# A second store buffer for the attended products of a scan, and their tiles beside its first six blocks

## The chip, the cores and the metric

The kernel runs on one core of a Trainium2 chip. A core has five engines that each work through a queue of their own in order: PE (matrix products), DVE (elementwise work), ACT (activations and copies), POOL (elementwise work and DMA issues) and SP (DMA issues). ACT, POOL and SP each issue DMAs, which run on 16 shared DMA engines. The metric is the device time of one execution in microseconds; the median of three runs stands for a kernel.

## The reference

One layer of a bidirectional encoder on 1024 tokens of width 1024, all in float32. It is two half-step FFNs around a mixer; the mixer projects the input once, gives one part of the columns to dilated window attention (8 heads of 64) and the other to a recurrent group (RWKV-7, 8 heads of 64, forward and backward), and projects both back with one matrix `w_out`:

```python
f = _swiglu(_rmsnorm(h, ffn1_pre_g), ffn1_w_gate, ffn1_w_up, ffn1_w_down)
h = h + 0.5 * _rmsnorm(f, ffn1_post_g)
z = _rmsnorm(h, mix_pre_g) @ w_in
y_att = _attention_group(z[..., :ATT_IN], cos, sin, attn_out_g)
y_rwkv = _rwkv7_group(z[..., ATT_IN:], ...)
mix = jnp.concatenate([y_att, y_rwkv], axis=-1) @ w_out
h = h + _rmsnorm(mix, mix_post_g)
f = _swiglu(_rmsnorm(h, ffn2_pre_g), ffn2_w_gate, ffn2_w_up, ffn2_w_down)
h = h + 0.5 * _rmsnorm(f, ffn2_post_g)
```

The recurrence per head, over time in both directions:

```python
sa = jnp.einsum('dbhvk,dbhk->dbhv', state, kk)
state = state * w[..., None, :] - sa[..., :, None] * kka[..., None, :] + v[..., :, None] * k[..., None, :]
y = jnp.einsum('dbhvk,dbhk->dbhv', state, r)
```

## The kernel before

The kernel runs through the first FFN, the input projection, attention, the recurrent scan, the output projection and the second FFN, in that order, with some work of one stage laid beside another. Products of float32 data are made of three matmuls of a high and a low part (`woh`, `wol` of the weights; `yah`, `yal` of the data), so one product of a 128-row tile with half the output columns takes 4 x 3 = 12 matmuls (`out_products`, L1064).

The scan takes the 1024 steps in 8 blocks, each of which holds two chunks of 64 steps for both directions. For block n there are four pieces of work:

- `prep` (L805 to L846) makes the operands of a block from loads (`th_w`, `th_a`, `in`), with products `lp` and `bp` on PE; it does not depend on the running state.
- `solve` (L854 to L873) inverts a small triangular matrix per head on DVE in 31 pairs of steps (L866, L868); its results `Ti` and `X` go to DRAM from POOL's queue.
- `merge` (L882 to L902) loads those inverses back on POOL's queue and joins them: `pa` on PE, its copies `d` on ACT, `pb` on PE, and the copy `tt` on ACT.
- `chain` (L928 to L972) carries the state through the block: copies `lm` on ACT (L928), then for each chunk `xu` (L941, L952), `xs` (L944), `uv` (L954), `st` and `y` on PE (L937), the new state `sv` on DVE (L968) and the output copy `yb` on ACT (L970). At the end ACT issues the two stores of `yb` to `d_y` (L972).

`run` issues merge(n), chain(n), and then prep and solve of a block three ahead (`upto(n + 3)`). Beside this, `project_attended` multiplies one tile of 128 attended rows with the attended half of `w_out`: load `yat`, scale it on DVE (L1072), transpose it on PE (`yq`, L1075), split it (L1077 on ACT, L1078 on DVE), and for each half of the output columns 12 matmuls `po`, a copy `yao` on ACT (L1083) and a store to the DRAM buffer `d_hp` on ACT's queue (L1084). `yq` and `po` share one bank of PSUM. The weights for it (`WA`) are read and split by `out_weights` in eight pieces of 128 x 512: a load `wor`, a scaled high part `woh` on ACT (L1054) and a low part `wol` on DVE (L1055). `wor` and `yao` are buffers of one tag, "wor", in one pool.

After the last chain, eight `finish_unit` calls (L991 to L1028) load the scan's results (`f_y`, `f_k`, `f_r`, `f_v`, `f_sg`), normalise them (`yc`, `var`, `rstd`, `bonus`, `gate` on PE) and split them. `out_weights` is called a second time for the other half of `w_out`, in another pool, and `out_project` adds the products `pw` (L1064) to the attended part, which it loads from `d_hp`. The second FFN follows.

The order of each engine's queue is set by a scheduler when the kernel is built: it takes the instructions as the program gives them and places them by priority and by the buffers that are free. So the place of a call in `run` and the number of buffers move instructions well beyond the lines themselves.

Of the kernel before, what the change touches and what calls it, by code (L numbers as in the profile page):

```python
# [10 lines left out]
F32 = mybir.dt.float32  # L11
# [8 lines left out]
NK, NT, NJ = D // 128, S // 128, DFF // 128  # L20
# [143 lines left out]
class _Kernel:  # L164
# [876 lines left out]
    def out_weights(self, p, k0, gain=None):  # L1041

        nc, W = self.nc, []
        for k in range(4):
            hl = []
            for dh in range(2):
                raw = p.tile([128, 512], F32, name="wor", tag="wor", bufs=1)
                self.load(raw, self.io["w_out"][0][(k0 + k) * 128:(k0 + k + 1) * 128, dh * 512:(dh + 1) * 512])
                h = p.tile([128, 512], F32R, name="woh", tag="woh", bufs=8)
                l = p.tile([128, 512], F32R, name="wol", tag="wol", bufs=8)  # L1050
                if gain is None:
                    self.split(h, l, raw)
                else:
                    nc.scalar.activation(h, raw, AF.Copy, scale=gain[:, k:k + 1])  # L1054
                    nc.vector.scalar_tensor_tensor(l, raw, gain[:, k:k + 1], h, op0=OP.mult, op1=OP.subtract)  # L1055
                hl.append((h, l))
            W.append(hl)
        return W
# [7 lines left out]
    def project_attended(self, p, c, psum, t, W, rs_a):  # L1066

        nc, V, A, T = self.nc, self.nc.vector, self.nc.scalar, self.nc.tensor
        rows = slice(t * 128, (t + 1) * 128)
        y = p.tile([128, H, 64], F32, name="yat", tag="yat")  # L1070
        self.load(y.rearrange("p a b -> p (a b)"), self.ya_d[rows, :])
        V.tensor_tensor(y, y, rs_a[:, t * H:(t + 1) * H][:, :, None].to_broadcast([128, H, 64]), op=OP.mult)  # L1072
        q = psum.tile([128, 4, 128], F32, name="yq", tag="eo")
        for k in range(4):
            T.transpose(q[:, k, :], y.rearrange("p a b -> p (a b)")[:, k * 128:(k + 1) * 128], self.ident)  # L1075
        h, l = (p.tile([128, 4, 128], F32R, name="ya" + c, tag="ya" + c) for c in "hl")
        A.activation(h, q, AF.Copy)  # L1077
        V.tensor_tensor(l, q, h, op=OP.subtract)  # L1078
        for dh in range(2):
            ps = psum.tile([128, 512], F32, name="po", tag="eo")  # L1080
            self.out_products(ps, W, dh, h, l, slice(0, 128))
            o = p.tile([128, 512], F32, name="yao", tag="wor", bufs=1)
            A.copy(o, ps)  # L1083
            self.nc.scalar.dma_start(self.hp_d[rows, dh * 512:(dh + 1) * 512], o)  # L1084

# [77 lines left out]
    def run(self):  # L1163
# [5 lines left out]
        with self.top as top:  # L1169
# [8 lines left out]
            with ExitStack() as st:  # L1178
# [39 lines left out]
                p = self.pool(st, "ffn1")  # L1218
# [66 lines left out]
            def upto(m):  # L1285
                while nxt[0] <= min(m, NB - 1):
                    n = nxt[0]
                    blk[n] = self.prep(n, sp, pp, (R0, R1, B0)[n % 3])
                    self.solve(n, sp)
                    nxt[0] += 1  # L1290
# [5 lines left out]
            for n in range(NB):  # L1296
                if n:
                    self.merge(n, blk[n], sc, pm)
                self.chain(n, blk.pop(n), sc, pc)
                upto(n + 3)  # L1300
                for t in ([0, 1] if n == 0 else [n + 1] if n + 1 < NT else []):
                    self.project_attended(eo, sc, pe, t, WA, rs_a)
            s_sr.close()
            s_pr.close()
# [27 lines left out]
            for j in range(2):  # L1332
                for n in (1, 2):
                    gate_up.ready[n, j] = self.halves(wf, self.slab(wf, gate_up.source(j, 0, n - 1), bufs=2, queue=nc.gpsimd),
                                                      bufs=4)
# [37 lines left out]
            with ExitStack() as st:  # L1373
# [12 lines left out]
                p, hand = self.pool(st, "ffn2"), self.pool(st, "hand3")  # L1386
# [49 lines left out]
```

## Time and profile before

| what | value |
|---|---|
| runs | 2370.75, 2369.18, 2369.29 us, median 2369.29 |
| span of the profiled execution | 2367.7 us |
| PE busy in it | 2212.2 us (93%) |
| DVE busy | 1782.8 us (75%) |
| ACT busy | 1034.4 us (44%) |
| the eight cycles of the scan, 1280 to 1594 us | 44.7, 53.5, 37.3, 44.3, 38.8, 33.1, 27.2, 35.1 us |
| first tail stretch, 1594 to 1650 us | 56.0 us |

The profile gives no time of the profiled execution apart from its span; the median of the runs is 1.6 us above it. A cycle is counted from the end of the last output copy (`yb`) of one chain to that of the next; cycle 0 begins at 1280 us. In the timelines a row reads: start in us, duration, engine and line, operation, output and input, and in brackets how long the engine had been idle and what released it. PE rows are pipelined, so the busy time of single matmuls can add up to more than the stretch that they take.

### The profile page before, as it was taken

The numbers are of one execution on the slowest core, as the hardware profiler recorded it, in microseconds if no ns is written. First come the engines' busy times: TensorE is split into PE (matmuls) and PEld (weight loads), VectorE is DVE, ScalarE is ACT, GpSimd is POOL, SyncE is SP. The second block draws the span as 40 slices with busy tenths as digits, with TensorE's granted clock in tenths as the row PEclk, the third lists the DMA queues.
The fourth block names the chain that finished last, engine by engine and source line by source line (L and its number), as shares of the span: only waits on it lengthen the run. The fifth ranks groups of instructions, "written<-read, shape, count | busy, mean of one in ns | idle before, by whom it ended". The sixth has DMA issues, their size and how long they took to land. (4 is left out here: it accounts for less than half of the span.)

```text
span 2367.7 us, 39507 instructions
## 1 busy us (share of the span) xinstructions
PE 2212.2 (93%) x14532; PEld 1784.9 (75%) x14532; DVE 1782.8 (75%) x2957; ACT 1034.4 (44%) x1958; POOL 608.7 (26%) x732
## 2 busy tenths in 40 slices
PE   6999999999999998999995889988799999999997
PEld 4788888878877676788774767765678888887886
DVE  8899999865676344667568767837889999987565
ACT  4322333354676413666545545445442333235453
POOL 6244443400000010111102242432334344441000
PEclk8999999999999998999996798989989999999999
DMA  5354445486652514322369676577534544447655
GB/s 156 107 174 151 170 146 170 167 266 193 220 185 98 193 42 134 91 81 71 94 161 223 165 183 176 151 208 256 178 95 168 174 167 154 169 153 265 195 188 181
DMA packets 359381, 386.04 MB, mean 163 GB/s; under 512 B 74258, under 2 KB 265618, under 8 KB 359188
## 3 DMA queue, kind: packets, MB, share of 16 engines
q1 hardware_dynamic: 308512, 276.43, 38.8%
q0 software_dynamic: 30320, 94.44, 11.3%
q10 hardware_dynamic: 20356, 12.66, 1.9%
q8 instruction: 114, 1.87, 0.3%
q14 instruction: 79, 0.65, 0.1%
HBM read 257.53 MB, written 125.89 MB: 162 GB/s over the span
## 5 line engine op out<-in xcount | busy, mean ns | idle before, releaser
L186 ACT ACTIVATE wh<-raw 128x512 fp32r<-128x512 f32 (+1 forms) x273 | 167.8, 626 | 264.1 <-DVE raw L62 95.0
L187 DVE TENSOR_TENSOR wl<-raw,wh 128x512 fp32r<-128x512 f32 (+1 forms) x273 | 277.6, 1020 | 3.1 <-ACT wh L186 2.0
L81 PE MATMUL gu<-xh,wh 128*128 128x512 f32 x704 | 277.9, 395 | 0.9 <-ACT xh L186 0.8
L81 PE MATMUL gu<-xl,wh 128*128 128x512 f32 x704 | 276.3, 393 | 0.0
L81 PE MATMUL gu<-xh,wl 128*128 128x512 f32 x704 | 276.2, 392 | 0.0
L415 PE MATMUL pd<-gl,gwh 128*128 128x512 f32 x616 | 240.4, 390 | 3.1 <-DVE gl L187 3.1
L415 PE MATMUL pd<-gh,gwh 128*128 128x512 f32 x616 | 239.6, 390 | 0.5 <-DVE row L86 0.5
L415 PE MATMUL pd<-gh,gwl 128*128 128x512 f32 x616 | 239.7, 389 | 0.0
L86 DVE TENSOR_TENSOR row<-gu,row 128x512 f32<-128x512 f32 x308 | 206.4, 682 | 23.2 <-PE gu L81 22.4
L187 DVE TENSOR_TENSOR gwl<-graw,gwh 128x512 fp32r<-128x512 f32 (+1 forms) x176 | 117.0, 667 | 129.7 <-ACT gwh L186 127.5
L116 POOL DMA_DIRECT2D d_hid<-row x154 | 84.7, 551 | 470.6 <-DVE row L114 444.2
L186 ACT ACTIVATE gwh<-graw 128x512 fp32r<-128x512 f32 (+1 forms) x176 | 101.4, 576 | 190.5 <-PE pd L415 162.2
L81 PEld LDWEIGHTS gu<-xh,wh 128*128 128x128 f32 x704 | 133.9, 190 | 29.5 <-ACT xh L186 2.0
L81 PEld LDWEIGHTS gu<-xl,wh 128*128 128x128 f32 x704 | 133.8, 190 | 27.9
L81 PEld LDWEIGHTS gu<-xh,wl 128*128 128x128 f32 x704 | 133.3, 189 | 27.5
L415 PEld LDWEIGHTS pd<-gl,gwh 128*128 128x128 f32 x616 | 115.6, 188 | 28.5 <-DVE gl L187 4.9
L415 PEld LDWEIGHTS pd<-gh,gwh 128*128 128x128 f32 x616 | 115.5, 188 | 25.6 <-DVE row L86 0.8
L415 PEld LDWEIGHTS pd<-gh,gwl 128*128 128x128 f32 x616 | 115.6, 188 | 23.8
L94 ACT ACTIVATE row<-row 128x512 f32<-128x512 f32 x44 | 27.9, 633 | 223.9 <-DVE row L86 216.4
L187 DVE TENSOR_TENSOR gl<-raw,gh 128x512 fp32r<-128x512 f32 x160 | 112.9, 717 | 15.7 <-ACT gh L186 15.4
L145 POOL TENSOR_TENSOR ws<-ws 128x512 f32<-128x512 f32 x88 | 114.4, 1300 | 1.2
L186 ACT ACTIVATE gh<-raw 128x512 fp32r<-128x512 f32 x160 | 98.0, 621 | 32.2 <-DMA raw<-in_ffn_w_down_dram 21.1
(356 smaller groups left out, 5353.4 us busy)
## 6 DMA issues: line engine op xcount, KB each, us to landing
d_hid<-row POOLq DMA_DIRECT2D x154, 256.0 KB, 2.5
graw<-d_hid SPq DMA_DIRECT2D x132, 256.0 KB, 3.0
raw<-in_ffn_w_gate_dram SPq DMA_DIRECT2D x88, 256.0 KB, 3.1
raw<-in_ffn_w_up_dram SPq DMA_DIRECT2D x88, 256.0 KB, 3.3
ws<-in_ffn_w_down_dram SPq DMA_DIRECT2D x88, 256.0 KB, 4.5
d_ws<-ws POOLq DMA_DIRECT2D x88, 256.0 KB, 2.3
raw<-d_ws SPq DMA_DIRECT2D x88, 256.0 KB, 2.7
raw<-in_ffn_w_down_dram SPq DMA_DIRECT2D x66, 256.0 KB, 3.3
```

The lines of the kernel that those rows point to most:

```text
L81: self.K.nc.tensor.matmul(ps, a[:, k, :], b[:, k, :], start=(k == 0 and i == 0), stop=(k == 3 and i == 2))
L86: add = lambda o, x: V.tensor_tensor(o, ps, x, op=OP.add)
L94: A.activation(y[:, 0], y[:, 0], AF.Silu)
L116: put = lambda n, y: G.dma_start(self.hid[n - 1, j // 2], y)
L145: G.tensor_tensor(o, a, b, op=OP.subtract)
L186: self.nc.scalar.activation(h, src, AF.Copy)
L187: (eng or self.nc.vector).tensor_tensor(l, src, h, op=OP.subtract)
L415: T.matmul(ps[x], a[:, ts], b, start=(m == 0 and k == 0), stop=(m == NM - 1 and k == 2))
```

## The change

The tag "wor" gets two buffers instead of one, at both places where it is used: the loads `wor` of the weights and the copies `yao` of the products. And the tiles of `project_attended` are issued behind other chains: before, tiles 0 and 1 behind chain 0 and tile n + 1 behind chain n, up to tile 7 behind chain 6; now tiles 5 and 6 go together behind chain 4, tile 7 goes behind chain 5, and none behind chain 6. The products themselves, their sizes and their number are the same.

```diff
@@ out_weights
-                raw = p.tile([128, 512], F32, name="wor", tag="wor", bufs=1)
+                raw = p.tile([128, 512], F32, name="wor", tag="wor", bufs=2)
@@ project_attended
-            o = p.tile([128, 512], F32, name="yao", tag="wor", bufs=1)
+            o = p.tile([128, 512], F32, name="yao", tag="wor", bufs=2)
@@ run
-                for t in ([0, 1] if n == 0 else [n + 1] if n + 1 < NT else []):
+                for t in {0: [0, 1], 1: [2], 2: [3], 3: [4], 4: [5, 6], 5: [7]}.get(n, []):
```

In the queues this moves instructions as follows. On ACT, between the last output copies of chain 6 (`yb`) and the first work of chain 7, before:

```order
L970 COPY yb<-y 128x4x64 x2
L972 DMA d_y_146<-yb 128x4x128
L972 DMA d_y_149<-yb 128x4x128
L1083 COPY yao<-po 128x512
L1084 DMA d_hp<-yao 128x512
L1083 COPY yao<-po 128x512
L1084 DMA d_hp<-yao 128x512
L928 COPY lm<-pr 64x8x64
L896 COPY d_15801<-pa 32x16x2x16 x2
L928 COPY lm<-pr 64x8x64 x3
```

On ACT at the same place, now:

```order
L970 COPY yb<-y 128x4x64 x2
L972 DMA d_y_146<-yb 128x4x128
L972 DMA d_y_149<-yb 128x4x128
L928 COPY lm<-pr 64x8x64
L896 COPY d_15801<-pa 32x16x2x16 x2
L928 COPY lm<-pr 64x8x64 x3
```

Both copies of tile 7 and both of their stores have left this place; they now stand behind chain 5.

On ACT in chain 5, from its first copies to the first work of its first chunk, before:

```order
L928 COPY lm<-pr 64x8x64
L896 COPY d_15139<-pa 32x16x2x16 x2
L1083 COPY yao<-po 128x512
L928 COPY lm<-pr 64x8x64
L1084 DMA d_hp<-yao 128x512
L928 COPY lm<-pr 64x8x64 x2
L840 COPY bt<-bp 128x2x256 x2
L902 ACTIVATE tt_12090<-pb 32x16x32 x2
L944 COPY xs<-xu 128x512
```

On ACT in chain 5, now:

```order
L928 COPY lm<-pr 64x8x64
L896 COPY d_15183<-pa 32x16x2x16 x2
L928 COPY lm<-pr 64x8x64 x3
L840 COPY bt<-bp 128x2x256 x2
L1083 COPY yao<-po 128x512
L1084 DMA d_hp<-yao 128x512
L1083 COPY yao<-po 128x512
L1084 DMA d_hp<-yao 128x512
L902 ACTIVATE tt_12090<-pb 32x16x32 x2
L944 COPY xs<-xu 128x512
```

A second copy of products stands there, and both are now right ahead of the copy `tt` of the merge.

On SP during chain 0, where the attended weights are loaded, before:

```order
L182 DMA wor<-in_w_out_dram 128x512
L823 DMA d_kd_140<-th_a 128x4x128
L182 DMA th_w<-d_w_110 128x4x128
L182 DMA X<-d_x_158 64x1024 x2
L182 DMA wor<-in_w_out_dram 128x512
L182 DMA th_a<-d_a_116 128x4x128
L182 DMA in_12716<-d_rk 128x12x128
L182 DMA wor<-in_w_out_dram 128x512 x3
L823 DMA d_kd_143<-th_a 128x4x128
L182 DMA in_13240<-d_rk 128x12x128
```

On SP at the same place, now:

```order
L182 DMA wor<-in_w_out_dram 128x512 x2
L823 DMA d_kd_140<-th_a 128x4x128
L182 DMA X<-d_x_158 64x1024 x2
L182 DMA th_w<-d_w_110 128x4x128
L182 DMA in_12716<-d_rk 128x12x128
L182 DMA th_a<-d_a_116 128x4x128
L823 DMA d_kd_143<-th_a 128x4x128
L182 DMA in_13240<-d_rk 128x12x128
```

The last four loads that stood behind this point have moved ahead of it: all eight are issued in pairs in front of the stores and loads of the next block.

Counted over PE's queue, the products of L1064 per cycle (0 to 7) are 6, 45, 24, 25, 20, 26, 33, 13 before and 8, 47, 28, 25, 29, 38, 17, 0 now. The transposed tiles `yq` fall into the cycles as 1, 2, 1, 1, 1, 1, 1, 0 before and 1, 2, 1, 1, 1, 2, 0, 0 now. Of the 192 products `pw` of the tail, 24 stand ahead of the last unit's `gate` before and 57 now.

## The prediction

> **What bounds the kernel now.** I read the page first, then a table of stretches over the scan, then the timelines of single engines at the two places where the table looks bad. The page says what kind of kernel this is:
>
> ```profile
> span 2367.7 us, 39507 instructions
> PE 2212.2 (93%) x14532; PEld 1784.9 (75%) x14532; DVE 1782.8 (75%) x2957; ACT 1034.4 (44%) x1958; POOL 608.7 (26%) x732
> PE 26%; DVE 2%; issue 1%; DMA 1%; ACT 0%; POOL 0%; SPq 0%; DVEq 0%; POOLq 0%
> ```
>
> The PE is nearly always occupied, and the chain of waits is mostly PE; but that chain is followed only through the second FFN, which the change does not touch. The change lives in the scan and in the tail behind it, so I cut the scan at the last output copy of each chain; the rows are cycles c0 to c7, and then the tail in two pieces.
>
> ```profile
> core 0: us, PE busy (x) PEld busy (x) DVE busy (x) ACT busy (x) POOL busy (x), PEclk, DMA share, GB/s
> 1280.00:1324.70 44.70, 28.01 (x506) 24.31 (x506) 30.45 (x83) 21.96 (x40) 16.90 (x29) 0.67 0.85 211
> 1324.70:1378.20 53.50, 46.32 (x603) 36.68 (x605) 39.46 (x120) 24.40 (x45) 16.37 (x28) 0.78 0.64 164
> 1378.20:1415.50 37.30, 34.22 (x593) 28.47 (x592) 23.93 (x62) 20.67 (x39) 12.38 (x21) 0.91 0.73 174
> 1459.80:1498.60 38.80, 33.89 (x589) 28.89 (x588) 33.04 (x102) 20.46 (x39) 13.03 (x22) 0.87 0.69 172
> 1498.60:1531.70 33.10, 31.91 (x586) 26.73 (x583) 26.05 (x78) 17.36 (x32) 13.07 (x22) 1.00 0.55 147
> 1531.70:1558.90 27.20, 25.82 (x502) 20.47 (x502) 18.48 (x62) 11.38 (x21) 13.57 (x22) 1.00 0.44 118
> 1558.90:1594.00 35.10, 26.67 (x494) 21.56 (x494) 5.75 (x13) 14.12 (x25) 12.11 (x13) 0.81 0.92 279
> 1594.00:1650.00 56.00, 45.98 (x191) 28.99 (x190) 38.36 (x65) 30.34 (x61) 13.88 (x11) 0.94 0.79 263
> ```
>
> c3 is left out. Three readings. c5 and c6 are bound by PE: 31.91 of 33.10 us and 25.82 of 27.20 us. c7, the last chain, has 8.4 us without PE work and fuller DMA (0.92) than any other row. c1 is the longest cycle and leaves PE idle for 7.2 us.
>
> In c7 the idle time is one wait. ACT, then PE:
>
> ```profile
> 1559.69 0.59 ACT L1083 COPY yao<-po 128x512 f32<-128x512 f32 x1 [0.85 <-ACT yb L970]
> 1570.41 0.59 ACT L1083 COPY yao<-po 128x512 f32<-128x512 f32 x1 [10.13 <-DMA d_hp<-yao]
> 1571.40 0.62 ACT L928 COPY lm<-pr 64x512 f32<-64x512 f32 x1 [0.41 <-ACT yao L1083]
> 1572.07 0.47 PE L941 MATMUL xu<-sv,lm 128*64 128x64 f32 x2 [6.81 <-ACT lm L928]
> 1577.90 2.08 PE L995 MATMUL yc<-f_y,k_cen 128*128 128x512 f32 x2
> ```
>
> The second half of tile 7 needs the only `yao` buffer, whose store lands 10.1 us after its issue. Behind that copy ACT holds the `lm` copies of chain 7, and PE stands for 6.81 us.
>
> **The change, part by part.**
>
> *The last gap (c7).* The four ACT rows ahead of `lm` are gone, and with them the 13 `po` matmuls that PE's queue has there. `lm` takes the place of the first copy, 1559.69, instead of 1571.40: 11.7 us earlier. What is late next?
>
> ```profile
> 1549.28 0.60 DVE L870 COPY X<-Ti 128x512 f32<-128x512 f32 x1
> 1557.87 1.30 POOL L886 DMA_DIRECT2D tt<-d_tt  x2
> 1558.65 1.00 SPq L182 DMA_DIRECT2D f_y<-d_y  x2
> 1568.60 1.25 POOL L994 TENSOR_TENSOR f_y<-f_y,f_y 128x512 f32<-128x512 f32 x1 [6.43 <-DMA d_hp<-yao]
> ```
>
> And how long stores of `yao` take over the scan:
>
> ```profile
> DMA to landing us min/median/max: 2.0/4.0/10.0
> ```
>
> The inverse of block 7 makes its round trip through DRAM: the last loads are issued until 1559.2, and by the lower half of those landings (2.0 to 4.0 us) they are there by about 1563, when `pa` and its copies are through as well. The first finish unit is the later one. Its `yc` stands in PE's queue ahead of chain 7's second products (L952), and it needs the sum on POOL, which ended at 1569.85 (the profile names the `yao` store as its releaser; the sum reads the loads of `f_y`, and I take those). If those loads do not land earlier, `yc` moves from 1577.90 to 1569.9, 8.0 us. I take -7; the ends are -3 (loads pushed into the same full DMA stretch give most of it back) and -10.1 (the whole wait).
>
> The Trainium skill ("DMA: Bandwidth & Descriptors", section "Anatomy of one DMA — SWDGE (gpsimd) path") fits a transfer as about 2.0 us fixed plus the bytes over 436 GB/s. For this 256 KB store that is an estimate of 2.6 us; the fastest landing (2.0 us) is near it, the one in the gap (10.0 us, at a DMA share of 0.92) is not. By the page the second copy would wait under 3 us and this term would be some -2 us.
>
> *c1.* It projects tiles 0 and 1 and in it the attended weights are still arriving, one buffer at a time. Waits over the scan (us in total, times, longest), and a row each of ACT and SP:
>
> ```profile
> ACT yao L1083 <- DMA d_hp<-yao: 14.4, 2, 10.1
> ACT woh L1054 <- DMA wor<-in_w_out_dram: 12.3, 4, 4.7
> SPq L182 <- DMA wor<-in_w_out_dram: 14.5, 4, 6.2
> 1364.66 0.59 ACT L1083 COPY yao<-po 128x512 f32<-128x512 f32 x1 [4.28 <-DMA d_hp<-yao]
> 1324.78 13.80 SPq L182 DMA_DIRECT2D wor<-in_w_out_dram  x3
> ```
>
> Behind the copy at 1364.66 stand chain 1's `uv` copies; behind the 13.80 us of SP stand the next block's loads. With two buffers the weights come in pairs, all eight issued within c0, and the 4.28 us wait goes. But PE idles only 7.2 us in c1, and c4, with no such wait, idles 4.9: the difference, 2.3 us, plus what a steadier PE gains in clock (46.3 us at 0.78 is 39.7 us at c2's 0.91, 6.6 less). Between 0 and -9 (2.3 + 6.6) I take the middle, -5. *c0* pays: some three of the eight 256 KB loads now run in it, 3 x 262 KB at its 211 GB/s is 3.7 us of a DMA that is free for 15%. Between 0 and +3.7 I take +1.
>
> *c2 to c6.* The order of the queues gives the products of each cycle; their price is the row of the cycle.
>
> ```profile
> 1378.20:1415.50 37.30, 8.58 (x24) 5.42 (x24) 0.91 0.73 174
> 1459.80:1498.60 38.80, 5.42 (x20) 3.52 (x20) 0.87 0.69 172
> 1498.60:1531.70 33.10, 7.88 (x30) 5.36 (x31) 1.00 0.55 147
> 1531.70:1558.90 27.20, 8.84 (x32) 5.28 (x30) 1.00 0.44 118
> 1531.70:1558.90 27.20, 0.65 (x4) 0.42 (x4) 0.69 (x1) 0.60 (x1) 1.00 0.44 118
> ```
>
> The first four rows are L1064 alone, the last one `yq`. c2 gets 4 more at 0.36 us = 1.4, with 3.1 us idle: +1. c4 gets 9 more at 0.27 = 2.4 with 4.9 idle: +1 (0 to +2.4). c5, bound by PE, gets 12 more at 0.263 and one more `yq`: 3.2 + 0.65 = +3.8, all on the path; two `yao` copies also stand just ahead of merge 5's `tt` copy on ACT. c6 loses 16 at 0.276 and its `yq`: -5.1 at most. Its chain's own latency isn't shown without products; the nearest is c7 from 1571.4 to 1594, 22.6 us, which allows -4.6. I take -4 (-2 to -5.1).
>
> *The tail.* The second use of the weights also gets two buffers, so its splits come earlier, and 57 of 192 `pw` matmuls, not 24, stand ahead of the last unit's gate.
>
> ```profile
> 1650.00:1710.00 60.00, 51.22 (x247) 41.26 (x245) 51.18 (x69) 31.03 (x63) 16.56 (x11) 0.99 0.56 181
> 1644.50:1661.00 16.50, 16.49 (x71) 13.43 (x72) 3.42 (x5) 1.00 0.70 233
> ```
>
> The second row is `pw` alone, behind that gate: they run back to back at 16.49/71 = 0.232 us; 33 of them are 7.7 us, moved into a stretch where PE idles 10.0 of 56.0 us. Behind it DVE is the dense engine (51.18 busy of the 60.00 us from 1650), which takes part of it back.
>
> I take -3 between 0 and -7.7. The loads and copies of a moved tile move with it, and the count of stores and bytes is unchanged: nothing is charged for those apart from the gap.
>
> Sum: +1 (c0) - 5 (c1) + 1 (c2) + 1 (c4) + 3.8 (c5) - 4 (c6) - 7 (c7) - 3 (tail) = -12.2 us. Against the profiled span that is 2355.5; the median of the runs, 2369.29, lies 1.6 us above the span, which gives 2357 us. A measurement here can tell about 0.2% (4.7 us) from no change: faster is below 2364.6, slower above 2374.0.
>
> **Rivals.**
>
> *The gap is handed on.* At 0.92 of DMA, what chain 7 gains is lost again by the finish units behind it, whose loads wait for the same 16 engines. For: the f_y sum waited 6.43 us for its data. Against: the two stores of 256 KB leave that stretch, and the tail's share is 0.79. The c7 term becomes -2, the tail 0: -4.2, or 2365 us.
>
> *The clock.* The products were filler between the chain's small steps. Without them PE falls to a lower clock in c6 and c7. Here are the same 32 products in chains 7 and 6:
>
> ```profile
> 1579.90 1.98 PE L952 MATMUL xu<-xs,tt 64*64 64x64 f32 x32
> 1553.67 1.10 PE L952 MATMUL xu<-xs,tt 64*64 64x64 f32 x32
> ```
>
> The slow one follows the stand of 6.81 us; the granted clock is 0.81 in c7 and 1.00 in c6. If c6 falls to 0.81, its remaining 21.4 us (25.8 - 4.4) become 26.4, +5.0; if c7 falls to c0's 0.67, its remaining 23.7 us become 28.6, +5.0. The sum is then -2.2: 2367 us. Against it: c7 loses its long stand, and the chain alone keeps PE busy in small steps. The Trainium skill ("TensorE: Matmul & The Clock Gate", section "What's actually happening") has the clock halve after a window of about 3.4 us without work and return after one of sustained work; the trace agrees with the first half, 1.98 against 1.10 us after 6.81 us idle. By that rule pauses shorter than the window cost nothing, and this rival would fall.
>
> *Slower: block 4 with two tiles delays the last inverse.* In c4 and c5 DVE carries the inverse of blocks 6 and 7 and now two tiles' scalings. What one tile could cost there:
>
> ```profile
> 1355.97 0.69 DVE L1078 TENSOR_TENSOR yal<-yq,yah 128x512 fp32r<-128x512 f32 x1 [3.32 <-ACT yah L1077]
> PE yq L1075 <- DVE yat L1072: 7.3, 1, 7.3
> ```
>
> DVE stood 3.32 us for the split's first half in c1, and 7.3 us is the longest that `yq` waited for its scaled tile. Two tiles at 3.32 + 7.3 are 21 us if all of it holds up the inverse and with it chains 5 to 7: 2357 + 21 = 2378 us. It decides from 12.2 + 4.7 = 17 us on. Against it: DVE is busy only 33.04 of 38.80 us in c4, and the order puts just one more pair of scalings there.
>
> That the change does nothing is excluded: the last copy before `lm` is gone from ACT's queue.
>
> **How the numbers follow.** The forecast as summed, 0.55; handed on, 0.17 (half of it under 2364.6); the clock, 0.13, within 0.2%; slower, 0.15. Faster: 0.55 + 0.09 + a little of the clock = 0.66; same 0.19; slower 0.15. All lower ends (0, -9, 0, 0, +3.8, -5.1, -10.1, -7.7) give -28 and 2341; all upper ones (+3.7, 0, +1.4, +2.4, +3.8, -2, -3, 0) +6.3 and 2376. Not all meet, so the range is 2346 to 2371; the forecast's own is 2347 to 2364.
>
> **What would show it.** In the changed profile: no wait for `d_hp<-yao` of over 1 us on ACT; chain 7's first `xu` within 3 us of chain 6's end, and 27 to 29 us for c7; c6 at 22 to 24 us with a clock above 0.9; c5 at 36 to 38 us; c1 under 50 us with no wait of `woh` above 2 us; the last gate's `pw` run about 7 us shorter. Wrong it would be if c4 and c5 together grow by over 10 us, if c7's first unit still starts `yc` 19 us after chain 6, or if the clock in c6 falls below 0.85.

## The result

The changed kernel takes 2356.93 us (median of four, 2354.73 to 2359.91) against 2370.02 us for the kernel before: a ratio of 0.9951, interval 0.9936 to 0.9965. Predicted were 2357 us. The number was met by luck: the profile shows that its terms were not met. The scan gained twice what the sum gave it, one cycle lost more than twice its share, and the tail moved the other way.

The profiled execution of the changed kernel, from the page:

```profile
span 2357.9 us, 39484 instructions
PE 2216.0 (94%) x14532; PEld 1788.8 (76%) x14532; DVE 1782.4 (76%) x2957; ACT 1035.0 (44%) x1958; POOL 609.7 (26%) x732
```

The same table of stretches, cut again at the last output copy of each chain. The rows are cycles c1 to c7 and the two stretches of the tail (last chain to the last unit's gate, and on to the first product of the second FFN):

```profile
core 0: us, PE busy (x) PEld busy (x) DVE busy (x) ACT busy (x) POOL busy (x), PEclk, DMA share, GB/s
1331.60:1372.30 40.70, 38.18 (x619) 31.16 (x617) 36.01 (x113) 22.70 (x42) 13.88 (x24) 1.00 0.76 202
1372.30:1410.50 38.20, 36.59 (x596) 29.42 (x596) 27.54 (x77) 20.71 (x40) 11.67 (x21) 0.87 0.71 187
1410.50:1444.30 33.80, 31.72 (x593) 26.37 (x591) 30.90 (x92) 21.25 (x41) 10.86 (x17) 1.00 0.84 216
1444.30:1484.90 40.60, 36.62 (x597) 30.34 (x595) 32.77 (x100) 20.72 (x40) 13.86 (x24) 0.87 0.66 172
1484.90:1526.10 41.20, 39.23 (x601) 31.28 (x600) 31.01 (x99) 18.46 (x35) 15.96 (x26) 0.92 0.53 139
1526.10:1548.10 22.00, 19.93 (x480) 16.54 (x479) 13.36 (x42) 10.87 (x20) 10.07 (x16) 1.00 0.44 112
1548.10:1578.20 30.10, 25.48 (x482) 20.10 (x483) 5.74 (x13) 12.91 (x23) 11.65 (x12) 0.77 1.00 301
1578.20:1634.00 55.80, 48.39 (x202) 32.81 (x201) 38.82 (x63) 28.73 (x59) 13.72 (x11) 0.91 0.77 257
1634.00:1675.00 41.00, 37.08 (x168) 29.17 (x166) 34.07 (x50) 21.05 (x44) 1.49 (x2) 0.96 0.50 167
```

c1 fell from 53.5 to 40.7 us and c3 from 44.3 to 33.8; c5 rose from 33.1 to 41.2; c6 and c7 fell by 5 each. The rows of the kernel before for c3 and for the same two stretches of its tail, which the prediction did not show:

```profile
1415.50:1459.70 44.20, 37.84 (x593) 30.68 (x591) 33.01 (x98) 20.64 (x39) 7.38 (x11) 0.81 0.66 163
1594.00:1644.80 50.80, 40.77 (x169) 24.95 (x168) 34.62 (x59) 28.46 (x57) 13.88 (x11) 0.93 0.80 264
1644.80:1687.00 42.20, 39.87 (x189) 32.08 (x188) 36.88 (x55) 23.58 (x48) 1.50 (x2) 1.00 0.55 186
```

In this pair of profiles the units before the last gate take 5.0 us longer, and the stretch behind it is only 1.2 us shorter, although the products in it became fewer.

The place of the 10.13 us wait, in the changed kernel. ACT, PE and POOL between chains 6 and 7:

```profile
1547.80 0.99 ACTq L972 DMA_DIRECT2D d_y<-yb  x2
1551.33 0.62 ACT L928 COPY lm<-pr 64x512 f32<-64x512 f32 x1 [3.29 <-PE pa L894]
...
1552.01 0.33 PE L941 MATMUL xu<-sv,lm 128*64 128x64 f32 x2 [0.15 <-ACT lm L928]
...
1558.37 1.11 PE L941 MATMUL xu<-sv,lm 128*64 128x64 f32 x14
1559.41 2.08 PE L995 MATMUL yc<-f_y,k_cen 128*128 128x512 f32 x2
...
1556.71 1.25 POOL L994 TENSOR_TENSOR f_y<-f_y,f_y 128x512 f32<-128x512 f32 x1 [5.82 <-DMA f_y<-d_y]
```

The copies and the wait are gone. `lm` now waits 3.29 us for the products `pa` of the merge, PE's first product of the chain comes 4.0 us after chain 6's end, and `yc` follows it at 11.4 us instead of 19.1. `yc` starts right behind `xu`; the sum on POOL had ended 1.45 us before.

One execution is not enough for all of this. The executions of one kernel differ by 10 us and more here (the kernel before took 2361.84 to 2379.61 us in 28 executions beside the first experiments), and the first load of the attended weights, in front of which nothing was changed, falls anywhere from 1279.8 to 1287.9 us in the fourteen profiles. That is why the cycles, which start afresh at each chain, are compared below over many profiles.

### The profile page after: what moved, and what is told of

Read it like the earlier page. It is cut to its first block, busy times and chain, and to the rows that moved or that the text cites. A ratio compares the mean times of both kernels' runs of the same rounds, so it can differ in the third digit from the quotient of the medians.

```text
span 2357.9 us, 39484 instructions
## 1 busy us (share of the span) xinstructions
PE 2216.0 (94%) x14532; PEld 1788.8 (76%) x14532; DVE 1782.4 (76%) x2957; ACT 1035.0 (44%) x1958; POOL 609.7 (26%) x732
## 3 DMA queue, kind: packets, MB, share of 16 engines
q1 hardware_dynamic: 308512, 276.43, 38.8%
## 5 line engine op out<-in xcount | busy, mean ns | idle before, releaser
L81 PEld LDWEIGHTS gu<-xh,wh 128*128 128x128 f32 x704 | 133.4, 190 | 30.2 <-ACT xh L186 2.8
L187 DVE TENSOR_TENSOR gl<-raw,gh 128x512 fp32r<-128x512 f32 x160 | 113.0, 717 | 17.5 <-ACT gh L186 17.2
```

Of the source, the lines that this page charges most:

```text
L81: self.K.nc.tensor.matmul(ps, a[:, k, :], b[:, k, :], start=(k == 0 and i == 0), stop=(k == 3 and i == 2))
L187: (eng or self.nc.vector).tensor_tensor(l, src, h, op=OP.subtract)
```

## The experiments

What each kernel shows, all in us. The ratio is to the kernel before, executed beside it; the cycles are from each kernel's own profile. "After the scan" is from the last chain's end to the end of the span.

| kernel | buffers in the scan | tiles | tail | ratio, interval | c1 | c3 | c5 | c6 | c7 | scan | after the scan |
|---|---|---|---|---|---|---|---|---|---|---|---|
| before | 1 | old | 1 | 1 | 53.5 | 44.3 | 33.1 | 27.2 | 35.1 | 314.2 | 773.8 |
| before_again | 1 | old | 1 | (one execution) | 51.7 | 44.5 | 33.1 | 27.3 | 37.0 | 309.6 | 774.7 |
| the change | 2 | new | 2 | 0.9951 (0.9936 to 0.9965) | 40.7 | 33.8 | 41.1 | 22.0 | 30.2 | 291.8 | 779.7 |
| again | 2 | new | 2 | 0.9961 (0.9943 to 0.9979) | 43.3 | 36.3 | 42.7 | 22.0 | 28.7 | 294.7 | 777.0 |
| buffers_only | 2 | old | 2 | 0.9945 (0.9928 to 0.9961) | 43.3 | 35.0 | 33.5 | 28.3 | 28.9 | 291.1 | 781.5 |
| tiles_only | 1 | new | 1 | 1.0000 (0.9979 to 1.0020) | 49.3 | 40.8 | 41.6 | 21.9 | 29.7 | 298.1 | 774.9 |
| tiles_only_again | 1 | new | 1 | (one execution) | 49.5 | 45.7 | 43.9 | 22.0 | 29.1 | 312.4 | 775.5 |
| tail_one | 2 | new | 1 | 0.9933 (0.9908 to 0.9958) | 43.7 | 34.8 | 40.5 | 22.0 | 30.1 | 291.5 | 772.6 |
| tail_one_again | 2 | new | 1 | 0.9953 (0.9926 to 0.9979) | 43.3 | 33.6 | 41.1 | 22.0 | 30.7 | 300.5 | 779.8 |
| scan_buffers | 2 | old | 1 | 0.9938 (0.9916 to 0.9960) | 40.8 | 36.3 | 35.3 | 28.3 | 30.2 | 298.9 | 773.4 |
| weights_two | weights 2, copies 1 | old | 1 | 1.0019 (1.0002 to 1.0035) | 44.5 | 40.7 | 36.7 | 28.4 | 30.8 | 314.5 | 770.1 |
| copies_two | weights 1, copies 2 | old | 1 | 1.0026 (1.0004 to 1.0047) | 47.9 | 42.0 | 37.1 | 28.9 | 29.7 | 312.9 | 769.8 |
| weights_pair | weights 2, copies 1 | old | 1 | 1.0036 (1.0014 to 1.0058) | 54.1 | 40.9 | 36.1 | 27.2 | 33.8 | 321.3 | 776.1 |
| copies_pair | weights 1, copies 2 | old | 1 | 1.0022 (1.0007 to 1.0037) | 47.5 | 34.5 | 40.9 | 29.4 | 30.5 | 307.8 | 771.8 |

### The change again, and the kernel before again

No edit. Expected:

> The changed kernel once more, for a closer interval and a second profile. Theory (the gain sits in the scan, and the first profile began its scan 6 us late by slower clock before it): a median of 2355 to 2358 us; the scan from the first load of the attended weights to the last output copy takes 290 to 294 us as in the first profile (291.8, before 314.2), the first output stretch of the scan begins 0 to 6 us earlier than in the first profile of the change. Rival (cycles 1 and 3 gained by a clock that happened to be high): the scan takes over 298 us this time.

> The kernel before once more, for a second profile. If the cycles are set by the order of the queues: cycle 1 at 49 to 54 us, cycle 3 at 40 to 45, cycle 7 at 34 to 36, the scan at 305 to 316 us. If cycle 1 and cycle 3 of the first profile were slow by chance: cycle 1 at 45 us or less or cycle 3 at 37 us or less.

The changed kernel took 2357.53 us (median of 12), and its scan 294.7 us, just over the 290 to 294 expected and clear of the rival's 298; the kernel before had its scan at 309.6 us in the second profile, with c1 at 51.7 and c3 at 44.5. So the long c1 and c3 belong to the kernel before, not to one execution of it. (Its c7, 37.0, is a little above what was expected.) With two profiles of each, the scan gains 18.7 us (311.9 to 293.2). Less than that arrives at the end: the medians differ by 11 to 13 us.

### Which part of the change

```diff
# buffers_only: the changed kernel with the tiles placed as before
-                for t in {0: [0, 1], 1: [2], 2: [3], 3: [4], 4: [5, 6], 5: [7]}.get(n, []):
+                for t in ([0, 1] if n == 0 else [n + 1] if n + 1 < NT else []):
# tiles_only: the kernel before with the tiles placed as in the change
-                for t in ([0, 1] if n == 0 else [n + 1] if n + 1 < NT else []):
+                for t in {0: [0, 1], 1: [2], 2: [3], 3: [4], 4: [5, 6], 5: [7]}.get(n, []):
```

> Only the two buffers, tiles placed as before. Theory (buffers carry cycle 1 and the wait in the last gap; the placement costs cycle 5 about what it gives cycle 6): cycle 1 at 41 to 45 us, cycle 5 at 33 to 35, cycle 6 at 27, cycle 7 at 30 to 32 because the second copy no longer waits for the first store; in all 2354 to 2360 us, about as fast as the full change. Rival (the empty last gap is what pays): cycle 7 stays at 33 to 35 us, and the time is 2361 to 2366 us.

> Only the placement of the tiles, one buffer. Theory (the buffers carry cycle 1): cycle 1 stays at 50 to 54 us, cycle 5 at 41 to 45 us with new waits of a copy for a store in cycles 4 and 5, cycle 7 at 30 us; in all 2366 to 2374 us. Rival (the placement alone pays): 2357 to 2362 us.

> The placement alone once more, for a second profile, since the first fell on the fastest of its twelve executions. Theory (no gain without the buffers): the scan at 305 to 315 us, cycle 1 at 49 to 54 us, cycle 5 at 41 us, cycle 6 at 22, cycle 7 at 30. Rival (the placement shortens the scan and the time is lost outside it): the scan at 296 to 301 us again.

The buffers alone give the whole gain: 2354.53 us. The placement alone gives nothing: 2369.61 against 2368.75 us beside it. The first profile of tiles_only fell on the fastest of its twelve executions (2354.81 us) and would have misled on the scan; the second, at 2371.15 us, has it at 312.4 us, as the theory had it.

c7 is 29 to 30 us in both, so the last gap can be closed in two ways, and the two don't add up. ACT there in buffers_only, where the two copies of tile 7 still stand between the chains, and in the second profile of tiles_only, where the copies have one buffer but have left the place:

```profile
1552.01 0.58 ACT L1083 COPY yao<-po 128x512 f32<-128x512 f32 x1 [1.84 <-PE po L1064]
1554.69 0.62 ACT L928 COPY lm<-pr 64x512 f32<-64x512 f32 x1 [2.10 <-PE pa L894]
```

```profile
1568.13 0.62 ACT L928 COPY lm<-pr 64x512 f32<-64x512 f32 x1 [3.29 <-PE pa L894]
```

In both, `lm` ends up waiting for `pa`. Either part removes the wait for the store, and doing both removes it once. What the placement then does by itself is to move products from c6 to c5, and no gain shows in it: c5 and c6 together take 60.3 and 60.4 us in the kernel before, 63.6 and 65.8 in the two profiles of tiles_only, 61.9 in buffers_only, and 63.1 and 64.7 in the two of the change.

### The tail's second buffer

```diff
# tail_one: the changed kernel, one buffer for the second use of out_weights
-                raw = p.tile([128, 512], F32, name="wor", tag="wor", bufs=2)
+                raw = p.tile([128, 512], F32, name="wor", tag="wor", bufs=1 if gain is None else 2)
# scan_buffers: the same edit on buffers_only
```

> The full change, but one buffer for the weights of the tail (the second use of out_weights). Theory (33 products moved between the finish units lengthen those units by about 5 us and shorten what follows by less): last chain to last gate 51 us instead of 55.8, in all 3 to 5 us less than the full change, 2352 to 2354 us. Rival (the longer units come from the clock or the loads, not from the products): within 1.5 us of the full change.

> Two buffers in the scan alone: the tiles placed as before, one buffer for the weights of the tail. Theory (the buffers of the scan are the whole gain; the placement gives cycle 6 what it takes in cycle 5, and the tail's second buffer costs about 5 us): cycles 5 to 7 at 33, 28 and 29 us, last chain to last gate about 51 us, in all 2346 to 2351 us, level with the full change with a one-buffer tail. Rival (the placement adds a gain of its own): 2353 us or more, slower than the run below by 3 us or more.

> The full change with one buffer for the tail's weights, once more, to compare with the run above: 2348 to 2353 us by both theories, cycles 5 to 7 at 41, 22 and 29 us.

The profiles speak one way: from the last chain to the end, the three profiles with two buffers in the tail take 779.7, 777.0 and 781.5 us, mean 779.4; the eleven with one buffer take 769.8 to 779.8, mean 773.9. So kernels with the second buffer take about 5.5 us more there, where the prediction had it give 3. PE's rows around the last gate, first the changed kernel, then tail_one:

```profile
1633.01 1.03 PE L1025 MATMUL gate<-f_sg,g2w 128*128 128x256 f32 x4
1675.28 1.45 PE L81 MATMUL gu<-xh,wh 128*128 128x512 f32 x4 [0.25 <-ACT xh L186]
```

```profile
1626.02 1.03 PE L1025 MATMUL gate<-f_sg,g2w 128*128 128x256 f32 x4
1668.94 0.39 PE L81 MATMUL gu<-xh,wh 128*128 128x512 f32 x1
```

The 5.5 us have three parts, in the means of the three profiles and of the eleven. From the last chain to the end of that gate it takes 55.9 us against 52.0, but the eleven spread from 48.7 to 57.0, and the second profiles of the changed kernel and of the kernel before both have 54.4: that the units in front of the gate are longer for the products moved into them is not shown. From the gate to the first product of the FFN it is 1.5 us shorter with the second buffer (in the rows above, from the gate's start, 42.3 and 42.9 us). From that product to the end it is 3.2 us longer, and this part is clear of the spread: 682.0 to 682.8 us in the three, 678.1 to 681.1 in the eleven.

So the moved products did not bring the next stage forward by what they took. In the kernel before, the last `pw` ends 4.2 us after the first product of the FFN; in the changed one it ends 2.2 us before it. But DVE adds in that last `pw` (L1095) only 3.9 us after its end in the one and 1.8 us after it in the other, and PE then waits for rows of DVE and POOL. PE's waits in the 60 us from the FFN's first product, first in the kernel before, where PE is busy for 43.2 of them, then in the changed kernel, where it is busy for 40.2:

```profile
PE pt L330 <- DVE row L266: 9.8, 3, 4.8
PE pt L330 <- POOL row L340: 5.2, 2, 2.9
```

```profile
PE pt L330 <- DVE row L266: 9.3, 3, 4.5
PE pt L330 <- POOL row L340: 7.5, 3, 2.8
```

PE waits there with or without the products beside it. Why the changed kernel takes longer from there on is open.

The times are less sure. The first six executions gave tail_one 2350.35 us against 2357.53 for the full change, ten more on another chip 2358.97; all 16 executions of tail_one have a mean of 2355.8, the 12 of the full change 2358.4, with standard errors of 1.6 and 1.3. scan_buffers against buffers_only (2354.9 and 2356.2) points the same way, no more strongly. Those ten were expected at 2348 to 2353 us and missed it. So did scan_buffers, expected at 2346 to 2351 and measured at 2354.88; that is the rival's time, but the rival also had it slower than tail_one beside it, and it was faster. So a one-buffer tail is not shown to be faster in time, and scan_buffers and tail_one, the lowest ratios here, are not told apart from the change itself. Nor is the placement, on top of the buffers, told from none: 2358.4 against 2356.2 in one set, 2357.8 against 2354.9 in the other.

### Weights or copies

Both share one tag. For a second buffer for one of them alone, the experiments borrow a buffer of another tile.

```diff
# weights_two: scan_buffers, but the copies go into the tile's own buffer
-            o = p.tile([128, 512], F32, name="yao", tag="wor", bufs=2)
+            o = p.tile([128, 512], F32, name="yao", tag="yat")
# copies_two: the kernel before, the second copy into the tile's buffer
-            o = p.tile([128, 512], F32, name="yao", tag="wor", bufs=1)
+            o = p.tile([128, 512], F32, name="yao", tag="yat" if dh else "wor", bufs=1)
```

> Two buffers for the attended weights in the scan; the copies of products have one buffer, now that of the attended tile (yat); tiles placed as before, one buffer in the tail. Theory (the pairs of weights carry cycle 1, the copies' second buffer carries cycle 7): cycle 1 at 41 to 45 us, cycle 7 back at 34 to 38 us with a wait of the second copy for the first store of 5 to 10 us; in all 2355 to 2360 us. Rival (the copies carry cycle 1 as well): cycle 1 at 48 us or more, in all 2363 us or more.

> One buffer for the attended weights; the two copies of a tile go to two buffers (one shared with the weights, one with the attended tile); tiles placed as before, one buffer in the tail. Theory: cycle 1 at 49 to 54 us with its waits for the weights, cycle 7 at 29 to 33 us without a wait of a copy for a store; in all 2358 to 2365 us. Rival (the copies carry cycle 1): cycle 1 at 45 us or less and 2352 us or less.

Both were slower than the kernel before (2374.52 and 2375.51 us) and missed what was expected of their totals. Borrowing `yat` was a fault of the design: a tile's attended rows can then not be loaded before the copies of the tile ahead are stored. SP's queue waits for those stores for 46.6 us in ten pieces in weights_two and 52.8 us in seven in copies_two over the scan, against 1.5 us in the kernel before; c4, 38.8 us before, takes 46.6 and 45.7. The second pair borrows what is free at that moment:

```diff
# weights_pair: the kernel before, every other piece of the scan's weights in the tile's buffer
-                raw = p.tile([128, 512], F32, name="wor", tag="wor", bufs=1)
+                raw = p.tile([128, 512], F32, name="wor", tag="yat" if gain is not None and dh else "wor", bufs=1)
# copies_pair: the kernel before, the second copy in the buffer of its split's high part
-            o = p.tile([128, 512], F32, name="yao", tag="wor", bufs=1)
+            o = p.tile([128, 512], F32, name="yao", tag="yah" if dh else "wor", bufs=1)
```

> The attended weights alone get a second buffer: every other piece is loaded into the buffer of the attended tile (yat), which is free until they are done. Copies of products, tail and placement as before. Theory (the pairs of weights carry cycle 1 and with it the order that follows up to cycle 3, the copies carry the last gap): cycle 1 at 41 to 46 us, cycle 3 at 34 to 38 us, cycle 7 at 33 to 36 us with the wait of the second copy for the first store, in all 2357 to 2363 us. Rival (the copies carry it, or both are needed): cycle 1 at 48 us or more and 2365 us or more.

> The copies of products alone get a second buffer: the second half of a tile is copied into the buffer of its split's high part (yah), which is done with by then. Weights, tail and placement as before. Theory: cycle 1 at 47 to 53 us, cycle 3 at 40 to 44 us, cycle 7 at 29 to 31 us without a wait for a store, in all 2361 to 2367 us. Rival (the copies carry it): cycle 1 at 45 us or less, 2358 us or less.

The theory failed on both totals: 2380.78 and 2371.82 us, ratios of 1.0036 and 1.0022, where 2357 to 2367 had been expected. c1 with the weights' pairs alone is 54.1 us, not 41 to 46. The last gap went as expected. ACT in weights_pair, whose copies have one buffer:

```profile
1583.43 0.59 ACT L1083 COPY yao<-po 128x512 f32<-128x512 f32 x1 [9.12 <-DMA d_hp<-yao]
1584.42 0.62 ACT L928 COPY lm<-pr 64x512 f32<-64x512 f32 x1 [0.41 <-ACT yao L1083]
```

Its c7 is 33.8 us; in copies_pair it is 30.5. In this pair c7 follows the copies. But the wait alone does not set c7. In weights_two the second copy waits too, as was expected, and c7 is 30.8 us, not the 34 to 38 expected:

```profile
1581.36 0.59 ACT L1083 COPY yao<-po 128x512 f32<-128x512 f32 x1 [6.89 <-DMA d_hp<-yao]
```

For c1 to c3 neither half of the pair does it. The stretches c1 and c3 of before_again, weights_pair and copies_pair:

```profile
1326.60:1378.30 51.70, 45.31 (x602) 36.17 (x603) 39.24 (x119) 24.24 (x45) 16.43 (x28) 0.80 0.66 173
1414.60:1459.20 44.60, 38.54 (x603) 31.44 (x605) 33.87 (x100) 20.71 (x40) 7.97 (x12) 0.81 0.62 159
```

```profile
1329.00:1383.10 54.10, 45.98 (x628) 36.94 (x627) 41.53 (x129) 22.94 (x44) 13.97 (x24) 0.87 0.66 171
1423.70:1464.60 40.90, 33.95 (x590) 27.71 (x590) 30.24 (x90) 20.66 (x39) 3.99 (x7) 0.92 0.61 161
```

```profile
1329.20:1376.70 47.50, 42.57 (x592) 34.49 (x594) 37.75 (x115) 23.65 (x44) 15.40 (x26) 0.78 0.67 175
1423.60:1458.10 34.50, 31.96 (x593) 26.74 (x591) 29.05 (x83) 20.81 (x39) 6.70 (x11) 1.00 0.74 194
```

c1 to c3 together take 135.1 and 132.5 us in the kernel before, 124.3 and 131.8 in tiles_only, 112.7 to 119.3 in the six profiles with two shared buffers, 126.0 and 129.0 with the halves borrowed the first way, and 135.6 and 128.9 the second way. weights_pair pays for its loan once more: tile 0 can be loaded only when the weights are done, and the products of its first two tiles, which stand in c0 and c1 before (6 and 45 in the rows), are all in c1 (52). What each half is worth without such a loan stays open; what is shown is that the two shared buffers gain about 17.5 us in these three cycles (133.8 to 116.3 in the means), and that no borrowed half gained more than 8.

## Why the prediction was right in its number

Point by point, with the mean of the two profiles of each kernel:

- *c1, predicted -5 between 0 and -9:* measured -10.6 (52.6 to 42.0). The mechanism was named, the size was not. The bound came from PE's idle time, 2.3 us, and from the clock that c2 had, 6.6 us. In the first profiles the idle time fell from 7.2 to 2.5 us and PE's busy time from 46.3 to 38.2, at a granted clock of 1.00, above c2's 0.91; in the second ones they fell from 6.4 to 2.2 and from 45.3 to 41.2, at 0.92. The prediction took the middle of its two bounds; the cycle went beyond the lower one, -9.
- *c3, predicted 0:* measured -9.4 (44.4 to 35.0). This is the step that failed. I charged c3 nothing because its products are the same 25; but the order of the queues changes from c1 on, and c3 of the kernel before lost time at a place that I did not read. There PE waited 5.5 us in one piece for DVE's `lm`; in the changed kernel it is 1.8 us in two. The first row below is c3 of the kernel before, the second of the changed one.

```profile
PE lp L830 <- DVE lm L832: 5.5, 1, 5.5
```

```profile
PE lp L830 <- DVE lm L832: 1.8, 2, 1.2
```

  In the kernel before, steps that stand ahead of `lm` in DVE's queue waited for loads: the scaling of the fifth attended tile, then the first step of an inverse.

```profile
1412.43 0.69 DVE L1072 TENSOR_TENSOR yat<-yat,rs 128x512 f32<-128x512 f32 x1 [4.39 <-DMA yat<-d_ya]
1417.38 0.19 DVE L866 TENSOR_TENSOR ttmp<-X,Ti 128x31 f32<-128x31 f32 x1 [3.05 <-DMA X<-d_x]
```

  In the changed kernel DVE's longest wait for a load there is this one, behind `lm` and for the tile after:

```profile
1430.72 0.69 DVE L1072 TENSOR_TENSOR yat<-yat,rs 128x512 f32<-128x512 f32 x1 [0.72 <-DMA yat<-d_ya]
```

  The many profiles agree. In the four of kernels with one buffer, DVE waits 4.4 to 6.2 us for the fifth tile, and SP issued its load 9.4 to 9.6 us ahead of c3. In the six with two shared buffers, no wait of DVE for a load, from 5 us ahead of c3 to its end, is longer than that 0.72 us, and SP issued that load 18.7 to 21.3 us ahead of c3. So an earlier place of that load goes with the shorter c3; no run moved it alone.

- *c0 +1, c2 +1, c4 +1:* measured +1.8, +1.3 and +1.2. These held.
- *c5, predicted +3.8:* measured +8.8 (33.1 to 41.9). The place was right, the price of one product was not. L1064 alone, c5 and c6 of the changed kernel:

```profile
1484.90:1526.10 41.20, 13.26 (x41) 8.29 (x42) 0.92 0.53 139
1526.10:1548.10 22.00, 3.66 (x15) 2.37 (x13) 1.00 0.44 112
```

  The 11 products more cost 5.4 us (13.26 - 7.88), as each took 0.32 instead of 0.263 us: the clock was 0.92, and the row of before had been taken at 1.00. Seven of them ran between 1488.3 and 1495.1 us, where the granted clock was 0.50 (3.72 us for the seven), as did the rest of the work in that stretch.
- *c6, predicted -4:* measured -5.3, with the granted clock still 1.00. The rival of the clock (c6 at 0.81) did not happen; c7 went from 0.81 and 0.72 in the two profiles to 0.77 and 0.88.
- *The last gap, predicted -7:* measured -6.6 (36.0 to 29.5). The size was near, and what was named as late next was not. `yc` was not held by the sum of `f_y`; it came behind the merge's products and the chain's own `xu`, at nearly the same moment. By the fit of the Trainium skill ("DMA: Bandwidth & Descriptors", section "Anatomy of one DMA — SWDGE (gpsimd) path") this term would have been an estimated -2 us. That section is on DMAs that gpsimd issues, and this store is issued by ACT. The runs do not agree with the estimate: the wait in the kernel before was 10.13 us in the first profile and at most 9.4 in the second, and c7 is 6.6 us shorter where it is gone. How much of that is the wait's alone stays open, since weights_two has a wait of 6.89 us and a c7 of 30.8. "Handed on" is not borne out: with the gap closed and one buffer in the tail (tail_one, tail_one_again, scan_buffers), what follows the scan takes 772.6, 779.8 and 773.4 us, against 773.8 and 774.7 in the kernel before.
- *The tail, predicted -3 between 0 and -7.7:* measured +4.1 (774.2 to 778.4, last chain to end). Here the sign was wrong. The products did leave the stretch behind the last gate, at the price computed (gate to last `pw` 46.5 to 38.8 us, 7.7 us), but the next stage is held up by other work: the first product of the FFN comes 1.4 us earlier behind the gate, and from that product to the end the changed kernel takes 3.0 us more. The other 2.4 us lie in front of the gate, within what the profiles of one kernel differ by.
- *The rival that was slower* (two tiles in block 4 delay the last inverse): c4 grew by 1.2 us and no such wait shows.
- *A sign of being wrong* was that c4 and c5 together grow by over 10 us. They grew by 9.9 us in the first profiles and by 10.1 in the means, through c5: the sign was at its line though the total was met.

So that -12.2 us were predicted and -13.4 measured between the mean spans is luck, a sum of errors that cancel: 15 us too little for c1 and c3, 5 us too little charged to c5, 7 us too much expected of the tail. And the change as described has two parts of which one, the placement, is worth nothing that these runs can show.

## What to carry to other kernels

When one wait can be closed in two ways, a second buffer for the copy or another place for it, price each alone: the second one then has only its costs left. A buffer that is shared by two streams in a queue-ordered program changes the order of all that follows, so look for the gain in later cycles too, at the loads that other engines wait for, and repeat a profile before believing a cycle. Work that is moved ahead of a gate gains only if what stands behind the gate is paced by it: read what the instructions of the next stage wait for.

## What the runs showed of the hardware

A good part of the gain in c1 to c3 goes with the granted clock: PE's busy time in them fell by 11.9 of 22.3 us in the first pair of profiles (118.4 to 106.5, for 1789 and 1808 recorded matmuls) and by 5.1 of 14.7 us in the second. The cycle in which PE waits less also gets its products at a higher clock (0.78 to 1.00 in c1; 0.92, 0.92 and 1.00 in the profiles of again, buffers_only and scan_buffers, 0.78 to 0.92 in those with one buffer or a borrowed half). So in c1 what was gained is more than the idle time that went (4.7 of 12.8 us in the first profiles), and a product added to c5 cost more than its row at full clock (0.32 us instead of 0.263).

The clock does not need a long pause to stay low. c1 of the kernel before, PE's longest wait and three stretches of about 3.4 us inside it:

```profile
PE lp L830 <- DVE lm L832: 2.1, 1, 2.1
```

```profile
1346.80:1350.20 3.40, 3.40 (x13) 0.50 0.71 150
1350.20:1353.60 3.40, 3.40 (x16) 0.50 0.00 0
1357.00:1360.50 3.50, 3.50 (x33) 1.00 0.65 200
```

No wait in the cycle is longer than 2.1 us. The granted clock reads 0.50 in every stretch from 1340.0 to 1353.6 us, with PE recorded as busy for 13.5 of these 13.6 us, before it came back. The Trainium skill ("TensorE: Matmul & The Clock Gate", section "What's actually happening") gives the two states that these rows show, and a window of about 3.4 us without work for the lower one. From that I had read that shorter pauses cost nothing; c1 speaks against that reading. What sets the clock in a mixed stretch is not settled by these runs.

The clock also differs between executions of one kernel, which makes one execution a poor witness. The fastest and the slowest of twelve executions of tiles_only, 2354.81 and 2376.81 us, have mean clocks of 0.969 and 0.954.
